# 60 drains on ScalarE and VectorE ahead of the first work of a row-normalising kernel

## The chip, the cores and the metric

One Trainium2 chip, one core. The metric is the device time of one execution in microseconds (us), less is better. Before: 241.33 us, median of 3 runs (240.67 to 241.34). All runs in this study are of the same (fast) state, with a granted clock of 1.0.

## The reference

```python
# x: 8 x 512 x 2048 float32, gamma: 2048 float32
x_rep = np.repeat(x, 2, axis=1)
rms = np.sqrt((x_rep ** 2).mean(axis=-1, keepdims=True) + 1e-6)
return ((x_rep / rms) * gamma[None, None, :]).astype(np.float32)
```

Each row is normalised, multiplied by gamma and written twice. So 33.6 MB are read and 67.1 MB are written.

## The kernel before

The rows are cut into eight tiles of 128 partitions x 4 rows. A tile has room for the 8 output rows; the 4 input rows are loaded into its second half. There is room for three such tiles (`bufs=3`). SyncE issues all loads and stores of rows. The first tile is loaded in four transfers of 1 MB, the others in transfers of 4 MB (the last in two of 2 MB), and a store is 8 MB (the last two are 4 MB).

```python
ctx.enter_context(tc.manual_schedule())
load(0, nc.sync, parts=K)                                    # K = 4
gamma_b = singles.tile([P, D], f32, name="gamma_b")
nc.scalar.dma_start(out=gamma_b[0:1, :], in_=gamma.partition_broadcast(1))
nc.gpsimd.partition_broadcast(out_ap=gamma_b[:], in_ap=gamma_b[0:1, :])
eps_t = singles.tile([P, 1], f32, name="eps_t")
nc.vector.memset(eps_t, eps)
load(1, nc.sync)
load(2, nc.sync)

for i in range(ntiles):                                      # ntiles = 8
    parts = 2 if i == ntiles - 1 else 1
    for k in range(0, K, K // parts):
        compute(i, k, k + K // parts)     # ScalarE: square, sqrt, copies; VectorE: scale, copy
        store(i, k, k + K // parts)
    if i >= 1 and i + 2 < ntiles:
        load(i + 2, nc.sync, parts=2 if i + 3 == ntiles else 1)
```

From tile 3 on a load waits until the store of the tile whose room it takes has finished (the trace of before has five such waits of SyncE, 37.0 us in all). So the data queue turns from store to load and back once per tile.

## Time and profile before

| | before |
|---|---|
| time | 241.33 us (240.67 to 241.34) |
| span of the profiled run | 238.8 us |
| ScalarE busy, VectorE busy | 48%, 38% |
| data queue, share of 16 DMA engines | 98.4% |

The first excerpt is from the page of the profile: the span; busy tenths in 40 slices of the span (9 is 90% or more) for VectorE (DVE), ScalarE (ACT) and the DMA engines, and what these moved; the DMA queues with packets and megabytes; the chain that ended last.

```profile
span 238.8 us, 298 instructions
...
DVE  0477749671000085500864017730167219900000
ACT  2998999970000299203991059900598059600000
...
DMA  7999998989899998999898999899998999898994
GB/s 263 432 447 439 439 439 351 527 351 527 351 406 428 439 483 364 428 439 527 351 527 351 439 439 517 362 417 417 439 483 384 401 431 519 373 505 362 439 428 198
...
q1 hardware_dynamic: 3024, 100.66, 98.4%
q14 instruction: 2, 0.02, 0.0%
...
DMA 66%; ACT 13%; DVE 7%; SPq 1%; issue 0%
```

The reader sees a kernel that is bound by its transfers: the DMA row is full from the second slice to the last but one, while the two engines that compute have long holes. `q14` is the queue that the page calls `instruction`; I take its packets for fetches of instructions. It has two in the whole span, 0.02 MB.

The next lines are the timeline of the first microseconds (start, duration, engine, what; in brackets how long the engine was idle before, and what ended that), and below it who SyncE's queue waited for (total, times, longest).

```profile
0.72 0.51 ACTq L97 DMA_DIRECT2D gamma_b<-in_gamma_dram  x1
0.72 3.06 SPq L52 DMA_DIRECT2D y<-in_x_dram  x6
...
1.27 1.28 ACT L64 ACT_TABLE_LOAD   x1 [1.27 <-PEq L125]
...
5.58 1.88 ACT L64 ACTIVATE sq<-y 128x2048 f32<-128x2048 f32 x1 [3.03 <-DMA y<-in_x_dram]
```

```profile
SPq L56 <- DVE y L80: 156.1, 9, 26.2
SPq L52 <- DMA out_dram<-y: 37.0, 5, 17.6
SPq L136 <- DMA out_dram<-y: 28.2, 3, 9.6
```

ScalarE sits idle for 3.03 us for the first megabyte; by my estimate from that, up to 3 us of other work put there would cost ScalarE nothing. SyncE waits long for compute before it issues a store, but the queue still has work then, as the full DMA row says. At the end (L136) it waits for the last stores alone.

One more record of the trace matters, which no view of the profile prints: every packet of every queue with its start, duration and size. The two packets of the instruction queue are 8192 bytes each, start at 90.7 and 148.9 us and take 0.31 and 0.32 us. At the first ScalarE has begun 62 of its instructions, at the second VectorE 62 of its own. So I take each packet for the next 8 KB of one engine's instructions, and call such 8 KB a page.

### The profile page before, as it was taken

The numbers are of one execution on the slowest core, as the hardware profiler recorded it, in microseconds if no ns is written. First come the engines' busy times: TensorE is split into PE (matmuls) and PEld (weight loads), VectorE is DVE, ScalarE is ACT, GpSimd is POOL, SyncE is SP. The second block draws the span as 40 slices with busy tenths as digits, with TensorE's granted clock in tenths as the row PEclk, the third lists the DMA queues.
The fourth block names the chain that finished last, engine by engine and source line by source line (L and its number), as shares of the span: only waits on it lengthen the run. The fifth ranks groups of instructions, "written<-read, shape, count | busy, mean of one in ns | idle before, by whom it ended". The sixth has DMA issues, their size and how long they took to land.

```text
span 238.8 us, 298 instructions
## 1 busy us (share of the span) xinstructions
DVE 90.8 (38%) x74; ACT 115.6 (48%) x121; POOL 2.5 (1%) x5
## 2 busy tenths in 40 slices
DVE  0477749671000085500864017730167219900000
ACT  2998999970000299203991059900598059600000
POOL 4000000000000000000000000000000000000000
DMA  7999998989899998999898999899998999898994
GB/s 263 432 447 439 439 439 351 527 351 527 351 406 428 439 483 364 428 439 527 351 527 351 439 439 517 362 417 417 439 483 384 401 431 519 373 505 362 439 428 198
DMA packets 3028, 100.69 MB, mean 422 GB/s; under 512 B 337, under 2 KB 337, under 8 KB 337
## 3 DMA queue, kind: packets, MB, share of 16 engines
q1 hardware_dynamic: 3024, 100.66, 98.4%
q14 instruction: 2, 0.02, 0.0%
q10 hardware_dynamic: 2, 0.01, 0.0%
HBM read 33.56 MB, written 67.11 MB: 422 GB/s over the span
## 4 chain that ended last, share of the span: by engine, by line
DMA 66%; ACT 13%; DVE 7%; SPq 1%; issue 0%
DMA y<-in_x_dram 39%; DMA out_dram<-y 27%; ACT sq L64 7%; DVE y L74 6%; ACT y L80 5%; ACT rms L68 1%; DVE y L80 1%; SPq L52 1%; DVE rstd L73 0%; SPq L56 0%
## 5 line engine op out<-in xcount | busy, mean ns | idle before, releaser
L64 ACT ACTIVATE sq<-y 128x2048 f32<-128x2048 f32 x32 | 59.9, 1872 | 85.8 <-DMA y<-in_x_dram 85.8
L74 DVE SCALAR_TENSOR_TENSOR y<-y,rstd,gamma_b 128x2048 f32<-128x2048 f32 x32 | 75.3, 2352 | 1.2
L73 DVE RECIPROCAL rstd<-rms 128x1 f32<-128x1 f32 x32 | 5.2, 162 | 116.1 <-ACT rms L68 116.1
L80 ACT COPY y<-y 128x2048 f32<-128x2048 f32 x23 | 43.4, 1888 | 3.6 <-DVE y L74 3.6
L80 DVE COPY y<-y 128x2048 f32<-128x2048 f32 x9 | 11.0, 1227 | 0.3
L68 ACT ACTIVATE rms<-ss,eps_t 128x1 f32<-128x1 f32 x32 | 9.4, 295 | 1.0
L64 ACT ACTIVATION_READ_ACCUMULATOR sq<-y 128x1 f32 x32 | 6.0, 186 | 0.0
L98 POOL PARTITION_BROADCAST gamma_b<-gamma_b x1 | 2.3, 2294 | 1.9 <-DMA gamma_b<-in_gamma_dram 1.9
L64 ACT ACT_TABLE_LOAD x1 | 1.3, 1283 | 1.3 <-PEq L125 1.3
L68 ACT ACT_TABLE_LOAD x1 | 1.3, 1283 | 0.0
L100 DVE MEMSET eps_t<- 128x1 f32 x1 | 0.1, 59 | 0.8 <-PEq L125 0.8
L125 POOL MEMSET const-float32-0.0<- 128x1 f32 x1 | 0.1, 100 | 0.2 <-issue 0.2
L125 POOL MEMSET const-bfloat16-1.0<- 128x1 bf16 x1 | 0.1, 102 | 0.0
L125 POOL MEMSET const-uint8-127<- 128x1 uint8 x1 | 0.1, 102 | 0.0
L125 POOL MEMSET const-float32-1.0<- 128x1 f32 x1 | 0.1, 99 | 0.0
## 6 DMA issues: line engine op xcount, KB each, us to landing
y<-in_x_dram SPq DMA_DIRECT2D x6, 4096.0 KB, 34.4
out_dram<-y SPq DMA_DIRECT2D x2, 4096.0 KB, 27.2
y<-in_x_dram SPq DMA_DIRECT2D x4, 1024.0 KB, 7.9
y<-in_x_dram SPq DMA_DIRECT2D x2, 2048.0 KB, 36.4
out_dram<-y SPq DMA_DIRECT2D x7, 31.7
gamma_b<-in_gamma_dram ACTq DMA_DIRECT2D x1, 8.0 KB
```

What stands on the lines that cost most here:

```text
L52: eng.dma_start(out=y[:, at : at + step, :], in_=x_t[i, :, k : k + step, :])
L64: nc.scalar.activation(out=sq[:], in_=ys[i][:, K * (R - 1) + k, :], func=Act.Square, accum_out=ss[:])
L68: nc.scalar.activation(out=rms[:], in_=ss[:], func=Act.Sqrt, scale=inv_d, bias=eps_t[:])
L73: nc.vector.reciprocal(out=rstd[:], in_=rms[:])
L74: nc.vector.scalar_tensor_tensor(out=ys[i][:, R * k, :], in0=ys[i][:, K * (R - 1) + k, :], scalar=rstd[:], in1=gamma_b[:], op0=Alu.mult, o ...
L80: copy(out=ys[i][:, R * k + 1, :], in_=ys[i][:, R * k, :])
L98: nc.gpsimd.partition_broadcast(out_ap=gamma_b[:], in_ap=gamma_b[0:1, :])
L100: nc.vector.memset(eps_t, eps)
L125: nc = _bacc.Bacc("TRN2", target_bir_lowering=False, num_devices=1)
```

## The change

The intent: use up the first page of each engine's instructions while it has nothing to do, so that the fetches that I take to come with the crossing into the next page happen at the start and not in the middle. That they go with an engine's count of instructions was inferred from the counts above; the runs below bear it out: with drains on ScalarE alone one fetch comes at 7.1 us, with drains on VectorE alone one at 6.9 us.

```diff
     nc.vector.memset(eps_t, eps)
+
+
+    for _ in range(60):
+        nc.scalar.drain()
+        nc.vector.drain()
     load(1, nc.sync)
     load(2, nc.sync)
```

A drain writes no tile. In the trace of before, the one at the end of the program starts on ScalarE 7 ns after the last copy starts and ends 37 ns after it ends: 1.93 us, beside a copy of 1.90 us.

## The prediction

> **What bounds the kernel now.** The transfers. The page's slices show the DMA engines at 8 to 9 tenths or more from the second slice to the last but one; the data queue is busy 98.4% of 16 engines' span, 422 GB/s. ScalarE is busy 48%, VectorE 38%; the chain of waits is 66% DMA. The packet records of the trace show about 434 GB/s sustained from 4 to 236 us; 100.7 MB at that rate need 232 us. Only a store issued after the queue has run dry can lengthen this.
>
> **What the change touches.** 60 drains on each of ScalarE and VectorE move the place where each crosses from one instruction page to the next. Before, the packet records have two 8192-byte packets of the instruction queue inside the span: at 90.7 us, when ScalarE is about at its 62nd instruction, and at 148.9 us, when VectorE is about at its 62nd; 0.31 us each. Neither shows as idle time: the table of waits gives all idle time of the two engines to loads and to each other. [...] Removed: nothing on the chain. Both fetches move to the first 3 to 6 us.
>
> **What it adds.** Sequencer instructions without work follow each other by 58 ns (SyncE's drains at the end) to 111 ns (VectorE at the end). Estimate from these: 60 drains cost 3.5 to 6.5 us per engine.
> - VectorE waits from 0.85 us to 9.2 us for the first rms: absorbed, unless the fetch stalls it.
> - ScalarE's gamma issue ends at 1.24 us; its first table load (1.28 us) probably comes after the drains; then the fetch, an estimated 0.5 to 2 us behind packets of 0.31 us if it isn't prefetched. First Square at 6 to 10.5 us instead of 5.58: 0.5 to 5 us late, most likely 2.
>
> **Is that on the critical path?** The delay goes through tile 0 nearly whole, so store 0 is issued at 24.5 to 29 us instead of 23.93. But the queue works on loads 0 to 2 until 33 us; the first store packet starts at 32.7 us, 8.7 us after its issue. Store 1 is issued at 39.8, while store 0 runs to 52.8; store 2 at 54.5 against 72.4. Each has more slack than the delay. From tile 3 on the engines wait for loads, and the delay is gone.
>
> **Predicted time: 241.2 us**, 8 in 10 within 240.3 to 242.4. Faster by over 2%: 0.01; within 2%: 0.97; slower by over 2%: 0.02.
>
> **What would show it.** Two instruction-queue packets inside the span, both within the first 8 us. First Square and first reciprocal 0.5 to 5 us later; first store's issue later by that; the end of loads 0 to 2 (33 us), the completion of store 0 (52.8 us) and all later landings within 0.5 us of before. DMA slices unchanged.
>
> **What would make it wrong.** A drain of 150 ns or more, or a page fetch of many us behind full rings at the start: then store 0 comes after 32 us, the queue runs dry, and the time grows by the excess. Or the fetches in mid-kernel hold a ring in a way I don't see; at most about 1 us.

One sentence is cut from it, where marked. It carried no term of the forecast's sum, which stands as recorded: 241.2 us. For the view that the two fetches cost nothing, the table of waits is what is left.

## The result, and the profile after

| | before | after |
|---|---|---|
| time, median (range) | 241.00 us (240.67 to 241.34), 4 runs | 242.82 us (242.69 to 243.23), 4 runs |
| ratio | | 1.0079, 95% interval 1.0055 to 1.0102 |
| span of the profiled run | 238.8 us | 240.9 us |

A ratio is the mean time of one kernel's fast runs over the mean of the other's of the same rounds, so not quite the ratio of the medians quoted. The change costs 0.8%: within 2%, but clear of noise, and outside the predicted range (240.3 to 242.4).

The same lines of the page, after:

```profile
span 240.9 us, 418 instructions
...
DVE  0477758771000066600746008540077309910000
ACT  2997999970000099401993039910499049700000
...
DMA  7999998989899989799989998989999899999991
GB/s 268 423 445 435 430 430 359 511 359 511 359 430 435 517 348 522 343 435 441 500 370 424 430 506 381 479 364 479 408 468 403 375 484 457 424 393 435 435 435 65
...
q1 hardware_dynamic: 3024, 100.66, 97.6%
q14 instruction: 3, 0.02, 0.0%
...
DMA 66%; ACT 13%; DVE 7%; SPq 1%; issue 0%
```

The last slice of the DMA row is 1 tenth instead of 4, and 65 GB/s instead of 198: the transfers have a longer tail. The timeline and SyncE's waits after:

```profile
0.72 0.52 ACTq L97 DMA_DIRECT2D gamma_b<-in_gamma_dram  x1
0.72 3.45 SPq L52 DMA_DIRECT2D y<-in_x_dram  x6
...
3.72 1.28 ACT L64 ACT_TABLE_LOAD   x1 [3.72 <-issue]
5.65 1.88 ACT L64 ACTIVATE sq<-y 128x2048 f32<-128x2048 f32 x1 [0.65 <-DMA y<-in_x_dram]
```

```profile
SPq L56 <- DVE y L80: 157.4, 9, 27.3
SPq L52 <- DMA out_dram<-y: 37.4, 5, 18.0
SPq L141 <- DMA out_dram<-y: 28.0, 3, 9.6
```

The drains themselves cost ScalarE nothing: the first Square starts at 5.65 instead of 5.58 us, because it still waits for data. In the trace the drains follow each other by 33 ns on ScalarE and 40 ns on VectorE. SyncE's waits differ by 1.3 us at most. So the engines don't explain 2.1 us of span.

The tail does. Each transfer of rows has 16 landings in the records, with their times, and the page counts 16 DMA engines. I call what leads to one landing a ring. The records carry no ring number, so which landings and packets of one transfer and the next are of the same ring is inferred from their times. The table is worked out from the records; times are from the start of the span.

```
                                   before                   after
landings of                first   median   last     first   median   last
1st load (1 MB)             5.06     5.21    5.56     4.99     5.19    5.63
2nd load (1 MB)             7.53     7.68    8.05     7.53     7.73    8.67
load 2                     33.00    33.23   33.43    32.91    33.20   34.76
load 3                     81.40    81.66   81.88    81.26    81.63   84.18
last store                236.11   236.58  237.88   236.07   236.62  239.99
```

At the last store the first and the middle ring end at the same time in both, to 0.05 us (over all transfers to 0.17 us). Only the latest rings differ. The last one decides: it ends 1.76 us after the first ring before, and 3.91 us after it with the change. That difference, 2.15 us, is the whole difference of the spans, 2.1 us. I call it the lag below: last landing minus first landing of one transfer.

The tail is to be seen in the windows of the last microseconds (columns: window, its length, busy time of VectorE, ScalarE, GpSimd, clock, DMA share, GB/s), before and then after. 66 GB/s over half a microsecond is one packet of 32 KB that started in it.

```profile
235.50:236.00 0.50, 0.00 (x0) 0.00 (x0) 0.00 (x0) 1.00 0.15 66
236.00:236.50 0.50, 0.00 (x0) 0.00 (x0) 0.00 (x0) 1.00 0.16 66
236.50:237.00 0.50, 0.00 (x0) 0.00 (x0) 0.00 (x0) 1.00 0.00 0
237.00:237.50 0.50, 0.00 (x0) 0.00 (x0) 0.00 (x0) 1.00 0.00 0
```

```profile
236.00:236.50 0.50, 0.00 (x0) 0.00 (x0) 0.00 (x0) 1.00 0.31 131
236.50:237.00 0.50, 0.00 (x0) 0.00 (x0) 0.00 (x0) 1.00 0.01 0
237.00:237.50 0.50, 0.00 (x0) 0.00 (x0) 0.00 (x0) 1.00 0.30 131
237.50:238.00 0.50, 0.00 (x0) 0.00 (x0) 0.00 (x0) 1.00 0.00 0
238.00:238.50 0.50, 0.00 (x0) 0.00 (x0) 0.00 (x0) 1.00 0.15 66
```

After the change two rings still send packets when fourteen have stopped: the other fourteen start their last 32 KB packet by 235.45 us, while two rows of packets, 1.21 us apart as each takes 1.21 us, go on at 236.01, 237.22 and 238.43 us, and at 236.28 and 237.49 us.

And where does the lag begin? Between the first and the second load, 0.63 to 1.13 us. These are packet records from there (from the start of the span, us; `q14` is the instruction queue; nominal is what an 8 KB packet of the same load takes otherwise, 309 ns):

```
7.11 to 7.42   8 KB  q14   309 ns
7.24 to 7.54   8 KB  q14   309 ns
7.43 to 8.08   8 KB  q1    658 ns  (309 nominal)
7.55 to 8.46   8 KB  q1    908 ns  (309 nominal)
```

The two page fetches are here, and the two data packets that start as they end take 349 and 599 ns too long. The records carry no ring number; that these packets are of the same rings is inferred from the times. The pattern comes back in the runs below: right after each fetch at about 7 us one such packet takes 574 ns (ScalarE alone), 858 (VectorE alone) and twice 856 (the changed kernel again). A third fetch comes at 214 us. ScalarE had begun 66 of its instructions at the first fetches and 191 at this one: 125 more. That it is ScalarE's is inferred too: with drains on ScalarE alone such a fetch comes (214.8 us), with drains on VectorE alone it doesn't.

The lag then grows: 1.12 us before the queue first turns from loads to stores (about 32 us), 1.85 after; 1.62 us before the second turn (81 us), 2.92 after. At the second turn a packet record shows how: one 32 KB load packet, from 80.34 to 82.63 us, took 2287 ns instead of 1213, while the other rings had all begun their store by 81.9 us. Other traces have such packets at a turn too, of 2051 ns with VectorE alone and 2165 ns with GpSimd. At the first turn it is less clear: there the last load packets of most rings take about 2.1 us, in the kernel before as well, and that of the late ring 2.65 us.

### The profile page after: what moved, and what is told of

It is laid out like the page before. It is cut to its first block, busy times and chain, and to the rows that moved or that the text cites. A ratio compares the mean times of both kernels' runs of the same rounds, so it can differ in the third digit from the quotient of the medians.

```text
span 240.9 us, 418 instructions
## 1 busy us (share of the span) xinstructions
DVE 90.8 (38%) x74; ACT 115.6 (48%) x121; POOL 2.5 (1%) x5
## 4 chain that ended last, share of the span: by engine, by line
DMA 66%; ACT 13%; DVE 7%; SPq 1%; issue 0%
DMA y<-in_x_dram 39%; DMA out_dram<-y 27%; ACT sq L64 7%; DVE y L74 6%; ACT y L80 5%; ACT rms L68 1%; DVE y L80 1%; SPq L52 1%; DVE rstd L73 0%; SPq L56 0%
```

## The experiments

The theory, H: a page fetch of 8 KB in the midst of the first loads makes one ring late by some tenths of a microsecond. Each later turn from load to store makes a late ring later, since its last load packet then runs beside the others' stores. The kernel ends with its latest ring. Rivals: the shifted engines (C), the program's length and place in memory (B), the drains as such (D), chance of one session (N), and a late ring that falls behind steadily (T). Chip sessions differ (the median of before was 241.78, 240.03, 240.56 and 240.79 us in the four sessions of the runs below), so each ratio is against runs of the kernel before on the same chip in the same session.

### Control: the kernel before again

No edit.

> The kernel before, unchanged, as a control. In the trace of the kernel before the sixteen landings of each transfer end within 0.5 us of each other at the first load and within 1.8 us at the last store; with the change within 3.9 us, while the median landing of the last store is the same (236.6 us in both). So the 1.8 us sit in one late DMA ring. Theory A (the change causes the lag of that ring): here 1.000 +- 0.002 of before and a spread of the last store's landings of 1.8 +- 0.5 us. Rival N (the lag is a property of one run or one chip, not of the kernel): the spread and the time differ from the first profile of the same kernel by 1 us or more.

Measured: 241.48 us (240.69 to 242.28), ratio 1.0002 (0.9971 to 1.0033). In the same rounds 11 runs of before lay between 240.07 and 242.41 us. The profiled run, 242.28 us, has a lag of 3.62 us; the first profile of before, of a run of 240.61 us, has 1.76. So rival N is half right: the kernel before scatters by 2.3 us, and between the two profiles the time goes with the lag too (1.67 and 1.86 us). The narrow range of its first three runs was luck. What remains for the change is that it puts all runs at the upper end.

### Only one engine

```diff
+    for _ in range(60):
+        nc.scalar.drain()          # the other run: nc.vector.drain()
```

> The 60 drains on ScalarE alone, VectorE as before. Theory A (page fetches at the start meet the data packets in one ring): one fetch early, one late; if ScalarE's early fetch is what counts, most of the 1.8 us stays; if both count, about half, 0.9 us (ratio 1.004). Rival B (any other program length shifts where things lie in memory): some other time, with no relation to which engine has the drains. Rival C (ScalarE's late start counts): whole loss here, none with VectorE alone.

> The 60 drains on VectorE alone, ScalarE as before. Theory A: about half of the loss (0.9 us, ratio 1.004), or all or nothing if only one engine's fetch matters; this and the ScalarE run should add up to the whole, 1.8 us. Rival C (ScalarE's late start): nothing, ratio 1.000. Rival B (program length): some time unrelated to that of the other run.

Measured: ScalarE alone 242.73 us (242.55 to 242.89), ratio 1.0055 (1.0031 to 1.0079), one fetch at 7.1 us. VectorE alone 242.69 us (242.40 to 242.97), ratio 1.0055 (1.0029 to 1.0082), one fetch at 6.9 us. Lags at the last store 3.65 and 3.95 us. I had expected the two to add up to the whole; each alone gives 0.55% of the 0.79%, with intervals that overlap that of the whole, and the same time within 0.15 us, though in another session. Rival C falls, since it expected no loss with VectorE alone. The landings say why there is no sum: in the kernel after, two rings are late (3.05 and 3.91 us), with one engine only one (the second is at 1.51 and 1.23 us). The end is the latest ring, a maximum, not a sum.

### The drains at the end of the program

```diff
             load(i + 2, nc.sync, parts=2 if i + 3 == ntiles else 1)
+    for _ in range(60):
+        nc.scalar.drain()
+        nc.vector.drain()
```

> The same 120 drains, but after the last work of ScalarE and VectorE, where both are idle for 28 us: same program length, page crossings in mid-kernel as before, nothing at the start. Theory A (early fetches): ratio 1.000 +- 0.002 and last-store spread near 1.8 us. Rival B (program length or placement): the loss stays, ratio near 1.008 and spread near 3.9 us.

Measured: 241.35 us (240.61 to 242.09), ratio 0.9999 (0.9970 to 1.0028). The time is that of before, and so is the scatter. The spread missed: the profiled run, at 242.09 us one of the slower ones, has 3.31 us and not 1.8, because before itself has such runs. The program's length alone shows no loss; rival B falls.

### The changed kernel again

> The changed kernel again, as a control, with more rounds. Runs so far: the kernel before scatters from 240.07 to 242.41 us, and its time follows the lag of its latest DMA ring at the last store (1.76 us lag in the 240.6 us run, 3.62 us in the 242.3 us run); with early drains on either engine or both all runs lie in 242.4 to 243.2 with lags of 3.65 to 3.95. Theory H: a page fetch of 8 KB in mid-load makes one ring about 0.5 us late, and every later turn from load to store makes a late ring later, until it saturates near 3.9 us; the kernel before gets such a seed later or smaller. Expected: 242.4 to 243.3, ratio 1.005 to 1.008, lag 3.6 to 4.0, two late rings. Rival N (chance of one session): scatter as wide as that of before.

Measured: 242.39 us (242.23 to 242.48), while before in the same session had 240.03 us (239.69 to 241.84); ratio 1.0079 (1.0052 to 1.0106), lag 3.66 us, second-latest ring 3.24. The changed kernel scatters by 0.25 us, before by 2.15. The loss is there again in another session and on another chip, so rival N falls for the change. The lag went so: 0.41 us at the first load, 1.09 at the second (fetches at 7.0 us in between), 1.12 to 1.70 at the first turn, 1.47 to 2.12 at the second, 1.89 to 2.40 at the third, 2.28 to 2.97 at the fourth; between turns, over the store, it shrank by 0.1 to 0.25 each time.

Not all of the end lag comes from the turns. Over the store in which ScalarE's next fetch comes (214.5 us), the lag steps from 3.15 to 3.69 us, and with ScalarE alone (214.8 us) from 3.09 to 3.69. In the first profile of after the second-latest ring steps from 2.49 to 3.07 there, and the latest only from 3.84 to 3.87. VectorE alone has no such fetch, and its lag goes from 3.86 to 3.90. So where ScalarE has the drains its next fetch adds 0.54 to 0.60 us to one of the late rings.

### The same dose without drains

```diff
     load(2, nc.sync)
+    nc.scalar.dma_start(out=ys[2][0:1, 0:1, :], in_=x_t[2, 0:1, 0:1, :])   # other run: 0:4, 32 KB
```

The rows written are overwritten later, before they are stored, so the result is right.

> No drains at all; one more 8 KB load of a single partition, issued by ScalarE right after its gamma load, into rows that nothing has written yet. It imitates the fetch: one 8 KB packet in one ring among the first loads. Theory H: as with the drains, one ring late by 0.3 to 0.6 us from the first loads on, lag of 3.6 to 4.0 at the last store, all runs in 242.4 to 243.2, ratio about 1.0055. Rival D (something of the drains themselves, their records or the engines' shifted instructions): like before, scatter 240.1 to 242.4, ratio 1.000.

> The same with 32 KB instead of 8: a dose four times as large, 1.2 us of one ring's time. Theory H with saturation near 3.9 us: ring late by about 1.2 to 1.5 us at once, lag at the last store 3.8 to 4.5, time 242.8 to 243.6. Theory H without saturation (fixed increments added to the seed): lag about 4.8, time 243.5 to 244. Rival D: like before, or 1.2 us over it at most.

Measured, 8 KB: 241.72 us (240.60 to 242.38), ratio 1.0050 (1.0018 to 1.0082). The mean moved as expected, the range did not: all six lie below the 242.4 us that I had named, and one is as fast as before. It is the profiled one, with a lag of 0.67 us already at the first load, 0.69 at the second and 1.87 at the end. So in that run the dose did not take. Measured, 32 KB: 242.42 us (242.10 to 242.79), ratio 1.0083 (1.0052 to 1.0114). Lag 0.40 us at the first load, 1.53 at the second, 3.53 at the end. No drain, no fetch at the start, and the loss is there: rival D falls. The dose is four times as large and the end lag not above that with the fetch (3.65 to 3.95 us), though I had expected 3.8 or more; in all full kernels profiled it stays below 4 us.

### Drains on an engine that has nothing to do

```diff
+    for _ in range(60):
+        nc.gpsimd.drain()
```

> 60 drains on GpSimd alone, after its only work; ScalarE and VectorE as before. GpSimd has nothing else to do, so no work is late. Theory H: if its page fetch falls into the first 20 us, its ring gets the same seed, and the time is again 242.4 to 243.2 (ratio 1.0055), with one early packet of the instruction queue in the span. Rival C (ScalarE or VectorE shifted) and rival D': ratio 1.000. If no fetch packet appears, it should be like before under H.

Measured: 241.98 us (241.61 to 242.16), ratio 1.0062 (1.0034 to 1.0089). One fetch at 13.3 us, beside those at 92.9 and 148.7 us. The lag is 0.30 us at the fourth load, 0.67 at the fifth (the fetch in between), 0.91 after the first turn, 1.43 after the second, 3.23 at the last store. ScalarE and VectorE have the program of before, and ScalarE's first table load comes after 1.3 us as there; GpSimd has no work after its drains. The fetch alone is enough.

### A later crossing

```diff
+    for _ in range(20):
+        nc.scalar.drain()
+        nc.vector.drain()
```

> 20 drains instead of 60 on both engines: the page crossings come at ScalarE's and VectorE's 43rd instruction of before, about 44 us and 91 us, instead of 7 us (60 drains) or 91 and 149 us (none). Theory H (a fetch makes a ring late, and each later turn from load to store adds to it): no lag over 0.8 us up to 33 us; the fetch at about 44 us falls among the 64 KB packets of a store; if it makes its ring late there, four or five turns are left and the lag ends at 2.5 to 3.9 us, time 1.003 to 1.006 of before. If a fetch among 64 KB store packets makes no ring late (in the runs of before none of the fetches at 91 us shows in the landings of 101 us), then like before, ratio 1.000 +- 0.003. Rival D (drains as such, whatever the fetch meets): a third of the loss, 1.002 to 1.003, and a lag from the first turn on.

Measured: 241.57 us (241.00 to 241.95), ratio 1.0037 (1.0008 to 1.0065). The fetches are at 32.6 and 90.6 us; I had put the first at 44 us, the time of ScalarE's 43rd or 44th instruction in before (42.5 and 44.3 us). It came when ScalarE had begun 52 instructions, against 60 to 66 in the other kernels; why so early is open. The time fits H and rival D alike. The profile is of the fastest run and shows 0.98 us after the first turn, 0.64 at the second turn and 2.30 at the end: the early fetch does not stand out. By itself this run decides nothing. Along with others it gives an order (fetches at 7 us 1.0079, at 13 us 1.0062, at 33 us 1.0037, at 91 us 1.000), but a weak one: the two runs with one fetch at 7 us gave 1.0055, in a session in which before was slower.

### The change, with the loads held back until the fetches are over

```diff
+    for _ in range(120):
+        nc.sync.drain()
     load(0, nc.sync, parts=K)
```

> The change as it is (60 drains on ScalarE and VectorE) and 120 drains on SyncE ahead of its first load, so that the loads start about 4 us later and the page fetches are over, or nearly over, before data move. Everything shifts by those 4 us. Theory H: the fetches meet no data packets and make no ring late: lag at the second load's landing under 0.8 us, at the last store as scattered as before (1 to 3.6 us), time 241 + 4 = 244 to 246 us, and the span from SyncE's first load to the end shorter than that of the changed kernel by 1 to 2 us in some of the runs. If the lag is 3.6 to 4 us in all runs, the meeting of fetch and data is not the cause.

```profile
0.72 0.50 ACTq L99 DMA_DIRECT2D gamma_b<-in_gamma_dram  x1
...
7.40 3.01 SPq L52 DMA_DIRECT2D y<-in_x_dram  x6
12.20 1.88 ACT L64 ACTIVATE sq<-y 128x2048 f32<-128x2048 f32 x1 [7.21 <-DMA y<-in_x_dram]
```

The lines are its timeline: SyncE's drains follow each other by 52 ns, with one longer step, of 0.40 us at 4.6 us, and the loads start 6.68 us later, not 4, so the time, 246.77 us (246.25 to 247.37), is over what I expected. The fetches are at 4.4 us (two) and 5.7 us (SyncE's own by my reading, since `q14` has four packets here and three in after); the first data packet starts at 8.4 us. The lag is 0.40 us at the second load, 0.55 at the second turn and 1.08 at the last store, the smallest of all full kernels profiled. Up to the sixth turn it lies between 0.39 and 0.70 us: here a ring that is not late to begin with is hardly made later. From first data packet to last landing it takes 235.2 us, against 236.1 in the first profile of before, and 238.2 in that of after. The drains, the page crossings and the fetches are all there, and more of them; what is gone is the meeting with data (that of gamma's single packet too, which had landed by 2.3 us), and the loss over before with it. One profile alone would not show that, since before scatters. But all five runs agree by an estimate from their spans: less the 9.4 us outside the data phase in the profile, 235.1 to 236.2 us; before in the same session, less its 2.7 us, 235.3 to 237.6. In the kernel after ScalarE's table load follows the last drain after 341 ns, where the drains follow each other by 33 ns; I take that for the step over the page end. The table load starts at 3.7 us here as there; the first fetch comes at 4.4 us here and at 7.1 us there, so with the loads ahead of it it is 2.7 us later.

### Gamma in pieces

```diff
-    nc.scalar.dma_start(out=gamma_b[0:1, :], in_=gamma.partition_broadcast(1))
+    nc.scalar.dma_start(
+        out=gamma_b[0:1, :].rearrange("p (a b) -> p a b", a=16),
+        in_=gamma.rearrange("(o a b) -> o a b", o=1, a=16),
+    )
```

> The kernel before, with gamma's 8 KB load written as 16 pieces of 512 bytes in the hope that they go to 16 rings; it is the only one-ring transfer that meets the first loads in the kernel before (one packet of 8 KB took 0.35 to 1.33 us at 1.6 us). If it is split, theory H expects the spread of the first landings to fall from 0.5-0.76 us to about 0.3 us and the time to 239.7 to 240.5 us in most runs, ratio 0.995 to 1.000. If the trace shows still one packet of 8192 bytes, the run says nothing and should be like before.

Measured: 239.96 us (239.77 to 241.10), ratio 0.9978 (0.9948 to 1.0009). The trace has still one packet of 8192 bytes, so the run says nothing; it is one more control.

### One turn only, without and with the drains

```diff
         if i >= 1 and i + 2 < ntiles:
-            load(i + 2, nc.sync, parts=2 if i + 3 == ntiles else 1)
+            ys.append(ys[i - 1])
```

The loads of tiles 3 to 7 are left out, the result is wrong. The second kernel has the change's 60 drains too.

> Wrong result on purpose: loads of tiles 3 to 7 left out, their compute and stores work on the old rows. The queue then moves 12.6 MB of loads, turns once to stores, and only stores 67.1 MB. No drains. At 434 GB/s these need 184 us; with 7 us of start and end about 191 us. Theory H (lag grows at each turn from load to store): one turn only, at about 32 us; lag at the last store under 1.1 us. Rival T (a late ring falls behind steadily, whatever moves): lag grows with time here too, 1.3 us or more.

> The same with the change's 60 drains on both engines; wrong result on purpose. Theory H: the fetches at 7 us make one or two rings late by 0.5 to 1.1 us, the one turn brings it to 1.1 to 1.9 us, and there it stays (1.0 to 1.9 us at the last store); the time is 0.3 to 1.1 us over the run without drains, against 1.8 to 2.4 us in the full kernel. Rival T: lag 3 us or more at the last store and 1.5 us or more over the run without drains.

Measured: 190.92 us (190.82 to 191.01) without drains, 191.99 us (191.85 to 192.30) with them: 1.07 us apart. The lags:

```
landings at about       5     7.5     22      33      52     110     129     149    187 us
without drains        0.53   0.50    0.52    0.60    0.62    1.15    1.11    1.07   1.00
with 60 drains        0.41   1.14    1.14    1.75    1.77    1.78    1.79    2.35   2.28
```

With the drains the lag jumps at the fetches (7.0 us), again at the one turn, and then stays within 0.04 us for nearly 100 us of stores. It doesn't creep; rival T falls. The one further step, 0.56 us, comes with ScalarE's next page fetch, at 147.8 us. Without drains the two steps, 0.62 to 0.87 and 0.83 to 1.15 us, lie where its fetches are (61.7 and 95.6 us). I had put the lag with drains at 1.0 to 1.9 us and had forgotten that third fetch. The windows of the end of the run with drains show its two late rings:

```profile
187.00:187.50 0.50, 0.00 (x0) 0.00 (x0) 0.00 (x0) 1.00 0.16 66
187.50:188.00 0.50, 0.00 (x0) 0.00 (x0) 0.00 (x0) 1.00 0.01 0
188.00:188.50 0.50, 0.00 (x0) 0.00 (x0) 0.00 (x0) 1.00 0.15 66
```

Without later turns the runs also stop scattering: 0.2 and 0.45 us instead of 2.

## Why the prediction was wrong

- **Bound by the transfers: right**, though at 430 GB/s by the packet records and not 434. But "only a store issued after the queue has run dry can lengthen this" was wrong: I treated 16 rings as one queue with one end. The kernel ends with the latest ring, and the mean rate (422 and 418 GB/s) doesn't tell how far that one is behind (1.76 and 3.91 us).
- **Engines absorb the drains: right, and by more than foreseen.** A drain took 33 to 40 ns and not 58 to 111; the step that I take for the crossing took ScalarE 341 ns; the first Square was 0.07 us late instead of 0.5 to 5. The slack of the stores that I worked out was never needed.
- **Fetches at the start: near in place, wrong in number.** Two came at 7.1 and 7.2 us (foreseen: 3 to 6, at most 8), and a third at 214 us, which comes with ScalarE's drains alone too and not with VectorE's.
- **The step that failed:** "Removed: nothing on the chain. Both fetches move to the first 3 to 6 us." I costed the moved fetch by the wait of the engine, "an estimated 0.5 to 2 us", and as traffic by its 0.31 us. Its cost to the ring that carries it was missing from the sum. Measured: 0.25 to 0.7 us more lag at once, grown to a lag of 3.65 to 3.95 us by the load-to-store turns that follow and, where ScalarE has the drains, by its next fetch at 214 us. And "all later landings within 0.5 us of before" holds for the first and the middle ring, to 0.17 us, and fails for the last, by 2.1 us at the last store.
- **What would make it wrong** named "the fetches in mid-kernel hold a ring in a way I don't see", with the sign reversed: fetches do hold a ring, but the early ones hurt more (0.25 to 0.7 us of lag at once, against 0.05 and 0.10 us at the fetches of before at 91 and 149 us). That this is because more turns follow them fits the kernels with one turn, and is not shown for each fetch.
- **The range** was too narrow for another reason: it rested on three runs of before that lay within 0.7 us. In more rounds before alone scatters from 239.6 to 242.4 us.

Shown: the place of the loss (latest ring), that a fetch that meets the first loads is enough (GpSimd), that an extra packet of 32 KB does it without drains (one of 8 KB did so in the mean, and not in the run profiled), that the loss goes when the fetches come before the data, and that over a long stretch of stores the lag holds still but for a further fetch. Inferred from times: which packets are of one ring. Open: why the data packet after a fetch takes twice to three times as long (658 and 908 ns against 309), why a load packet of a late ring took 2287 ns instead of 1213 beside the others' stores, and what starts the lag in the slower runs of the kernel before. The one profiled had 0.76 us at the first load; the slower run with the drains at the end had 0.47, no fetch before 90 us, and still ended at 3.31. So an early fetch is not needed for the lag; but with one or two at 7 us every run was slow (242.23 to 243.23 us).

No version here beats both kernels: holding the loads back frees 0.9 to 3.0 us of the data phase, by the two comparisons above, and costs 6.7.

## What to carry to other kernels

Here every transfer of rows had 16 landings, and the program ended with the latest of them (at 237.88 of 238.8 us before, at 239.99 of 240.9 after): look at the last slice of the DMA row and at the spread of the landings, not only at the mean rate. Small transfers of one packet (instruction pages, a gamma row) were cheap here ahead of the first data (a lag of 1.08 us at the last store), and dear among the first loads with six turns from loads to stores to follow (3.91 us with two fetches, 3.53 with an extra load of 32 KB). Late in the program it depended on the ring: the fetches at 91 and 149 us hardly moved the latest landing of the kernel before (0.48 to 0.53 and 0.76 to 0.86 us), but one at 148 or 214 us added 0.54 to 0.60 us to a ring that was late already. Here the idle time was free for the engine only: ScalarE's first Square came 0.07 us later, but the fetches that came with the drains cost 0.8% of the time.
